# Head sums with a stationary selector in four column groups, and both directions' rates on two row halves

## The chip, the cores and the metric

The kernel runs on one core of a Trainium2 chip. It is one program for the whole inference step, launched once. The metric is the device time of one execution in microseconds (us): 2121.82 us is the median of three runs of the kernel before (2121.23 to 2124.61). The engines are called PE (TensorE, matrix multiplication), DVE (VectorE), ACT (ScalarE), POOL (GpSimd) and SP (SyncE, which here only starts transfers).

## The reference, cut to what matters

The program computes a two-layer trunk over 640 tokens (128 of context and 512 latent ones) of width 1024: layer 0 mixes tokens by attention and a state-space scan, layer 1 by RWKV-7 time mixing, and each is followed by a gated feed-forward block. The change lies in layer 1, in the part that makes the inputs of the recurrent scan. Cut to that:

```python
k  = einsum('btd,de->bte', xk, w_k)                    # xk, xw, xa, xr, xg, xv: six mixes of neighbouring tokens
kk = split_heads(k * k_k)                              # 16 heads of 64 channels
kk = kk * rsqrt(sum(kk * kk, axis=-1) + 1e-12)         # unit keys: one sum per token and head
a  = sigmoid(a0 + einsum(einsum(xa, a1), a2))          # rates, for both directions (j = 0, 1)
k_dir = split_heads(k * (1 + (a - 1) * k_a))           # a key per direction
r  = einsum('btd,de->bte', xr, w_r)
bonus = sum(r * k_dir * r_k, axis=(direction, -1)) * v # the other sum per token and head
```

The two sums over the 64 channels of a head are called head sums here: sums of squares (norms) and bonus sums. There are 16 heads, so a tile of 128 channels holds two.

## The kernel before, in words

Tokens lie along the free axis: an activation is eight tiles of 128 channels by 640 tokens, and a matmul moves at most 512 columns, so the 640 tokens go in two blocks of 320 (`BLK`). The program is written in a tile framework: the kernel text allocates tiles from pools of fixed depth, a scheduler decides the order of instructions on each engine (it is not the written order), and each engine runs its own list in order, with semaphores between them. An fp32 matmul is two instructions on PE, so counts in the trace are twice those of the code.

The stage around the change has five parts, one behind the other on PE:

- Keys (lines 1309 to 1337). For each of eight channel tiles `dense` (line 401) makes k in 48 matmuls of 320 columns: the inputs are split into a high and a low part in a shorter format, so three products for each of eight inputs and two blocks. ACT copies the result out of PSUM twice, as `ks` (line 1318) and, scaled, as `kk` (line 1319), and squares kk into `sq` (line 1320). The norms of the tile before (`norms`, line 1305) are five matmuls: the squares of 128 tokens are the stationary operand, 128x128, and a selector with two columns (`sel2`: head 0, head 1) is moved. So the sums land with tokens on partitions, as `rsqrt` on DVE needs them. Between these stand matmuls of line 1267, a low-rank projection for the rates and then for the decays.
- Decays (line 1410): ten matmuls of 512 columns for direction 0, each read by a sigmoid on ACT (line 1411) and sent to DRAM. The mixes for the next projection are made meanwhile (`mix`: ACT line 1241, DVE lines 1242 and 1246, and `split`: ACT line 435, POOL line 436).
- r and rates (lines 1421 to 1442). For each tile `dense` makes r; `rates` of the tile before spreads the reciprocal norm over the channels (line 1374, stationary `sw`), multiplies (DVE line 1375), makes a for direction 0 and then for direction 1 (line 1381: contraction over 64 rows, rows 0 to 63 of `a2` and `ha` for direction 0, 64 to 127 for direction 1), applies tanh (ACT line 1385), sends keys to DRAM and leaves r times k_dir in `ks` (DVE line 1396). `bonus` (line 1401) takes the tile before that one: five matmuls with `ks` stationary and two columns of `srk` moved, all sums in one PSUM tile that DVE copies to `bon` at the very end (line 1463).
- Gate (line 1456): 16 matmuls of 320 columns, each pair copied by ACT and sent to DRAM.
- V projection (line 1709) and the scan. `right.close()` (line 1464) ends the life of the stage's pools. The scan's tile `ta` takes over SBUF that `ks` had, so its first writes (the load of constants, memsets, the loads of decays and keys) wait until the last reader of `ks` is done. The matmuls of the V projection fill PE while the scan is prepared.

PSUM is eight banks here: one for head sums (`ps_n`), one for transposes (`pg`), two for low-rank sums and four for the rest. `tmp()` gives one of four SBUF buffers of 128x640; `sw` has one.

Of the kernel before, what the change touches and what calls it, by code (L numbers as in the profile page):

```python
# [9 lines left out]
F32 = mybir.dt.float32  # L10
# [8 lines left out]
NT = 640  # L19
# [6 lines left out]
BLK = ((0, 320), (320, 640))  # L26
# [62 lines left out]
def _build(ctx, tc, I, O):  # L89
# [1105 lines left out]
    if True:  # L1195
# [91 lines left out]
        V.tensor_scalar(kac, vcol('rwkv_k_a', 0, 8), -1.0, 2.0, op0=ALU.mult, op1=ALU.add)  # L1287
        srk = l1a.tile([128, 8, 2], F32, name="srk")
# [7 lines left out]
        pn = ps_n.tile([128, 512], F32, name="pn", tag="n")  # L1296
# [6 lines left out]
        def norms(sq, m):  # L1303
            for b in range(5):
                T.matmul(pn[:, b * 16 + m * 2:b * 16 + m * 2 + 2], sq[:, b * 128:(b + 1) * 128], sel2, start=True, stop=True)
# [5 lines left out]
        for m in range(8):  # L1311
# [9 lines left out]
            if sqs:  # L1321
                norms(*sqs.pop())
            sqs.append((sq, m))
# [12 lines left out]
        norms(*sqs.pop())  # L1336
# [5 lines left out]
        a0c = l1a.tile([16, 128], F32, name="a0c")  # L1342
        load(a0c, I['rwkv_a0'][0].rearrange("d (k p) -> (d k) p", p=128))
        a0h = l1a.tile([128, 16], F32, name="a0h")

        def unit_keys():
            rkk = tmp("rkk")[:, 0:80]
            rsqrt(sqp, rkk, pn[:, 0:80], 80, 1.0, 1e-12)
# [20 lines left out]
        def rates(m, kt):  # L1369
# [7 lines left out]
            kds = []  # L1377
            for d in range(2):
                pa = [pd.tile([128, 512], F32, name=f"pa{b}", tag="d") for b in range(2)]
                for b, (c0, c1) in enumerate(BLK):  # L1380
                    T.matmul(pa[b][:, 0:320], a2[64 * d:64 * d + 64, m * 128:(m + 1) * 128], ha[64 * d:64 * d + 64, c0:c1],
                             start=True, stop=True)
# [16 lines left out]
        def bonus(m):  # L1399
            for b in range(5):  # L1400
                T.matmul(pnb[:, b * 16 + m * 2:b * 16 + m * 2 + 2], ks[:, m, b * 128:(b + 1) * 128], srk[:, m, :], start=True, stop=True)
# [21 lines left out]
        for m in range(8):  # L1423
# [7 lines left out]
            if m == 0:  # L1431
                selh, rk2 = unit_keys()
                pnb = ps_n.tile([128, 512], F32, name="pn", tag="n")
                gate = lora1(lora_in('rwkv_g1', 1), 5)
            else:
                if done:
                    bonus(done.pop())
                done.append(rates(*kts.pop(0)))
            for _ in range(2):
                next(dec, None)  # L1440
# [20 lines left out]
        for m in done:  # L1461
            bonus(m)
# [488 lines left out]
```

## Time and profile before

| | |
|---|---|
| median of three runs | 2121.82 us |
| profiled execution: its time, its span | 2116.96 us, 2115.2 us |
| mean granted TensorE clock | 0.943 |
| PE busy | 1950.7 us, 92% of the span |
| PE weight loads busy (beside PE) | 1785.1 us, 84% |
| DVE, ACT, POOL busy | 1447.0, 940.2, 560.6 us (68%, 44%, 27%) |
| the changed stage | 957 to 1260 us from the span's start |

The profile is one execution. A merged row of the timeline gives its start, the sum of the busy time of the instructions in it, the engine, the line, the operation with output and inputs, shapes, and their count; in brackets, how long the engine was idle before and which work ended that. Ends of matmuls are modelled and overlap the next start, so the price of a group on PE is read from its start to the start of the next group. The rest of the program is not touched.

### The profile page before, as it was taken

The page shows a single profiled execution, that of the slowest core. Times are in us where ns is not written, and L with a number is a line of the kernel's source. Part 1 is how long each engine was busy: PE and PEld are TensorE (multiplying, and loading weights), DVE is VectorE, ACT ScalarE, POOL GpSimd, SP SyncE. Part 2 cuts the span into 40 slices and gives each one's busy share as a digit, 9 for nine tenths or more (in the row PEclk, how much of TensorE's full clock was granted, in tenths as well). Part 3 has the DMA queues.
Part 4 walks back from the last instruction along what each step waited for, and adds up shares of the span by engine and source line. Part 5 has one row for each costly group of instructions (what it writes and reads, how often), then busy time and mean ns, then how long its engine had stood idle before and what let it go on. Part 6 is the DMA issues. An engine that isn't in the chain of part 4 may idle for free. (4 is left out here: it accounts for less than half of the span.)

```text
span 2115.2 us, 42931 instructions
## 1 busy us (share of the span) xinstructions
PE 1950.7 (92%) x17701; PEld 1785.1 (84%) x17701; DVE 1447.0 (68%) x2589; ACT 940.2 (44%) x1734; POOL 560.6 (27%) x510
## 2 busy tenths in 40 slices
PE   6999988999999999989999897877789999999998
PEld 5888766989999999969677786867779899999998
DVE  4474666467666758587676839889956787666675
ACT  4333454253433525355555343544463535344351
POOL 2111331002424326031234123313321025243330
PEclk8999999999999999989997988878889899999999
DMA  9764000422433524342466634425344322323221
GB/s 295 220 201 115 7 1 21 149 90 81 130 120 90 162 67 121 108 122 65 148 206 224 202 105 134 123 78 152 100 141 123 120 81 80 100 66 95 61 90 50
DMA packets 256408, 245.72 MB, mean 116 GB/s; under 512 B 27850, under 2 KB 217299, under 8 KB 256085
## 3 DMA queue, kind: packets, MB, share of 16 engines
q1 hardware_dynamic: 233076, 208.87, 32.9%
q0 software_dynamic: 5856, 21.01, 3.0%
q10 hardware_dynamic: 17280, 13.11, 2.0%
q8 instruction: 139, 2.28, 0.5%
q14 instruction: 57, 0.46, 0.1%
HBM read 203.76 MB, written 39.19 MB: 115 GB/s over the span
## 5 line engine op out<-in xcount | busy, mean ns | idle before, releaser
L979 DVE TENSOR_TENSOR ol<-wr,oh 128x512 fp32r<-128x512 f32 x344 | 316.1, 935 | 101.0 <-ACT oh L978 93.6
L978 ACT CAST oh<-wr 128x512 fp32r<-128x512 f32 x344 | 211.3, 619 | 307.1 <-PE d L1130 174.7
L1130 PE MATMUL d<-hid,oh 128*128 128x320 f32 x1312 | 291.3, 310 | 3.6 <-ACT hid L1027 2.5
L1130 PEld LDWEIGHTS d<-hid,oh 128*128 128x128 f32 x1312 | 220.5, 188 | 5.2 <-ACT hid L1027 3.2
L1130 PE MATMUL d<-hid,ol 128*128 128x320 f32 x656 | 203.0, 309 | 0.0
L443 DVE SCALAR_TENSOR_TENSOR x<-d,mod,x 128x128 f32<-128x128 f32 (+2 forms) x204 | 77.2, 433 | 141.6 <-PE d L1130 116.1
L1000 POOL TENSOR_TENSOR g<-wr 128x512 f32<-128x512 f32 x36 | 48.4, 1344 | 460.0 <-DMA wr<-in_ffn_w_up_dram 280.8
L1130 PEld LDWEIGHTS d<-hid,ol 128*128 128x128 f32 x656 | 123.6, 188 | 0.0
L401 PE MATMUL d<-hh,wh 128*128 128x320 f32 (+1 forms) x464 | 118.7, 328 | 3.5 <-ACT hh L435 1.6
L401 PE MATMUL d<-hl,wh 128*128 128x320 f32 (+1 forms) x464 | 114.2, 317 | 3.8 <-POOL hl L436 3.2
L401 PE MATMUL d<-hh,wl 128*128 128x320 f32 (+1 forms) x464 | 112.9, 315 | 0.0
L388 DVE TENSOR_TENSOR wl<-wr,wh 128x1024 fp32r<-128x1024 f32 (+1 forms) x57 | 70.1, 1230 | 56.9 <-ACT wh L386 56.4
L386 ACT CAST wh<-wr 128x1024 fp32r<-128x1024 f32 (+1 forms) x57 | 58.8, 1035 | 105.1 <-PE d L401 65.7
L401 PEld LDWEIGHTS d<-hh,wh 128*128 128x128 f32 (+1 forms) x464 | 79.7, 190 | 17.2 <-ACT at L1385 4.1
L401 PEld LDWEIGHTS d<-hl,wh 128*128 128x128 f32 (+1 forms) x464 | 79.2, 189 | 8.5 <-POOL hl L436 5.9
L1027 ACT CAST hid<-e 128x320 fp32r<-128x320 f32 x88 | 40.5, 460 | 101.4 <-DVE e L1045 100.9
L401 PEld LDWEIGHTS d<-hh,wl 128*128 128x128 f32 (+1 forms) x464 | 79.2, 189 | 1.6 <-DVE wl L388 0.6
L1534 PE MATMUL pS<-ar,ta 64*128 64x128 f32 x640 | 56.4, 311 | 21.4 <-POOL uv L1602 10.2
L1003 POOL TENSOR_TENSOR wr<-wr 128x512 f32<-128x512 f32 x36 | 50.6, 1409 | 84.9 <-DVE ol L979 57.0
L1534 PEld LDWEIGHTS pS<-ar,ta 64*128 64x128 f32 x640 | 48.5, 213 | 28.6 <-POOL uv L1602 11.1
L1005 POOL TENSOR_TENSOR wr<-wr 128x512 f32<-128x512 f32 x36 | 53.3, 1492 | 66.4 <-DVE ol L979 66.4
L1562 DVE TENSOR_TENSOR xt__11664<-ta 128x31 f32<-128x31 f32 (+15 forms) x155 | 66.4, 429 | 4.4 <-ACT ta L1760 0.2
(630 smaller groups left out, 5997.5 us busy)
## 6 DMA issues: line engine op xcount, KB each, us to landing
wt<-in_mod_w_dram SPq DMA_DIRECT2D x80, 512.0 KB, 4.3
wr<-in_ffn_w_gate_dram SPq DMA_DIRECT2D x44, 512.0 KB, 4.4
wr<-in_ffn_w_up_dram SPq DMA_DIRECT2D x44, 512.0 KB, 5.2
wr<-in_ffn_w_down_dram SPq DMA_DIRECT2D x44, 512.0 KB, 4.2
ta<-kbd SPq DMA_DIRECT2D x10, 1024.0 KB, 6.2
ar<-rkd SPq DMA_DIRECT2D x20, 512.0 KB, 5.6
wr<-in_ab_w_in_dram SPq DMA_DIRECT2D x16, 512.0 KB, 7.1
wt<-in_mod_w_dram SPq DMA_DIRECT2D x6, 1024.0 KB, 8.9
```

The costliest lines, as they stand in the source:

```text
L386: S.copy(wh, wr)
L388: V.tensor_sub(wl, wr, wh.bitcast(F32))
L401: T.matmul(ps[b][0:cn, 0:320], w[:, k, 0:cn], a[:, t0:t1], start=(k == 0 and i == 0), stop=(k == w.shape[1] - 1 and i == 2))
L443: V.scalar_tensor_tensor(out=x[:, k, c0:c1], in0=ps[b][:, c0 - 320 * b:c1 - 320 * b], scalar=mod[:, layer, v, gcol + k:gcol + k + 1], in1= ...
L978: S.copy(hi, src)
L979: V.tensor_tensor(out=lo, in0=src, in1=hi.bitcast(F32), op=ALU.subtract)
L1000: E.tensor_tensor(out=g3, in0=a11, in1=a21, op=ALU.add)
L1003: E.tensor_tensor(out=a11, in0=a11, in1=a21, op=ALU.add)
L1005: E.tensor_tensor(out=a12, in0=a12, in1=a11, op=ALU.add)
L1130: T.matmul(bank[:, 0:c1 - c0], p, q, start=i == 0 and z == 0, stop=i == n - 1 and z == 2)
L1534: T.matmul(pS[i][:, m], bk[r, g4 * 4 + m, :], ar[r, g4 * 4 + m], start=True, stop=True)
L1562: V.tensor_tensor(out=tv, in0=nu[:, j + 1:32, j:j + 1].to_broadcast([128, n, j + 1]), in1=wu[:, j:j + 1, 0:j + 1].to_broadcast([128, n, j ...
```

## The change

Head sums are turned round. `head_sums` makes the sums of four channel tiles at a time. The stationary operand is a selector padded to 32 columns (`sel32`; for the bonus `sr`, four such selectors with r_k in them); the data are moved, 320 columns at a time; the four tiles go to four column groups of the array (`tile_position=(0, 32*i)`), that is to partitions 0, 32, 64 and 96 of one PSUM bank. The sums then lie with heads on partitions, so ACT copies the bank to SBUF (`hs`), five transposes bring tokens back onto partitions, and two DVE copies pick the two real rows of every 32 and write them straight to `bon`; `pn` is now a view of `bon` in SBUF. It runs four times: norms after key tiles 3 and 7, bonus after five rates and at the end. The four squares of a group are kept in all four `tmp` buffers until then. `rates` allocates the PSUM tiles of both directions first and issues block 0 of both directions, then block 1 of both. The load of `a0c` moves into `unit_keys` and into a `tmp` buffer.

```diff
@@ -1285,6 +1285,9 @@
 
         kac = l1a.tile([128, 8], F32, name="kac")
         V.tensor_scalar(kac, vcol('rwkv_k_a', 0, 8), -1.0, 2.0, op0=ALU.mult, op1=ALU.add)
+        sel32 = l1a.tile([128, 32], F32, name="sel32")
+        G.memset(sel32, 0.0)
+        V.tensor_copy(sel32[:, 0:2], sel2)
         srk = l1a.tile([128, 8, 2], F32, name="srk")
         V.tensor_tensor(out=srk, in0=sel2.unsqueeze(1).to_broadcast([128, 8, 2]),
                         in1=vcol('rwkv_r_k', 0, 8).unsqueeze(2).to_broadcast([128, 8, 2]), op=ALU.mult)
@@ -1293,16 +1296,28 @@
 
         ks = l1b.tile([128, KT, NT], F32, name="ks")
         kk = xp.tile([128, KT, NT], F32, name="kk", tag="x")
-        pn = ps_n.tile([128, 512], F32, name="pn", tag="n")
+        pn = bon.rearrange("p b h -> p (b h)")
         ha = sqp.tile([128, NT], F32, name="ha", tag="ha", bufs=1)
         hw = [sqp.tile([128, NT], F32, name=f"hw{d}", tag="hl", bufs=2) for d in range(2)]
         for d in range(2):
             G.memset(hw[d][64:128, :], 0.0)
             G.memset(hw[d][64:65, :], 1.0)
 
-        def norms(sq, m):
-            for b in range(5):
-                T.matmul(pn[:, b * 16 + m * 2:b * 16 + m * 2 + 2], sq[:, b * 128:(b + 1) * 128], sel2, start=True, stop=True)
+        def head_sums(q, rows, dst, sums):
+
+
+            hs = sqp.tile([128, NT], F32, name="hs", tag="kt") if dst is pn and sums[0] is sel32 else tmp("hs")
+            for c0, c1 in BLK:
+                pb = ps_n.tile([128, 512], F32, name="pn", tag="n")
+                for i, (a, w) in enumerate(zip(rows, sums)):
+                    T.matmul(pb[32 * i:32 * i + 32, 0:320], w, a[:, c0:c1], start=True, stop=True, tile_position=(0, 32 * i))
+                S.copy(hs[:, c0:c1], pb[:, 0:320])
+            for b0, b1 in ((0, 4), (4, 5)):
+                pt = pg.tile([128, 512], F32, name="pt", tag="g")
+                for b in range(b0, b1):
+                    T.transpose(pt[:, (b - b0) * 128:(b - b0 + 1) * 128], hs[:, b * 128:(b + 1) * 128], ident)
+                V.tensor_copy(dst.rearrange("p (b m i) -> p b m i", b=5, i=2)[:, b0:b1, 4 * q:4 * q + 4],
+                              pt[:, 0:(b1 - b0) * 128].rearrange("p (b m r) -> p b m r", m=4, r=32)[:, :, :, 0:2])
 
         low = None
         nxt = mix(0, (hq, hp))
@@ -1318,9 +1333,10 @@
                 S.copy(ks[:, m, c0:c1], ps[b][:, 0:320])
                 S.activation(kk[:, m, c0:c1], ps[b][:, 0:320], AF.Copy, scale=vcol('rwkv_k_k', m))
             S.activation(sq, kk[:, m, :], AF.Square)
-            if sqs:
-                norms(*sqs.pop())
-            sqs.append((sq, m))
+            if len(sqs) == 4:
+                head_sums(0, sqs, pn, [sel32] * 4)
+                sqs = []
+            sqs.append(sq)
             for _ in range(2):
                 lps = next(low)
             if m == 3:
@@ -1333,19 +1349,19 @@
             if 1 <= m < 5:
                 take(nxt, (nhis, nlos), 1)
         take(nxt, (nhis, nlos), 4)
-        norms(*sqs.pop())
+        head_sums(1, sqs, pn, [sel32] * 4)
         his, los = nhis, nlos
 
 
 
         a2 = lora2(((0, 128, I['rwkv_a2'][0].rearrange("d r c -> (d r) c")),))
-        a0c = l1a.tile([16, 128], F32, name="a0c")
-        load(a0c, I['rwkv_a0'][0].rearrange("d (k p) -> (d k) p", p=128))
         a0h = l1a.tile([128, 16], F32, name="a0h")
 
         def unit_keys():
+            a0c = tmp("a0c")[0:16, 0:128]
+            load(a0c, I['rwkv_a0'][0].rearrange("d (k p) -> (d k) p", p=128))
             rkk = tmp("rkk")[:, 0:80]
-            rsqrt(sqp, rkk, pn[:, 0:80], 80, 1.0, 1e-12)
+            rsqrt(sqp, rkk, pn, 80, 1.0, 1e-12)
             pt = [pg.tile([128, 512], F32, name="pt", tag="g") for _ in range(1)]
             rkt = tmp("rkt")[0:16]
             for b in range(4):
@@ -1375,11 +1391,14 @@
                 V.tensor_tensor(out=kk[:, m, c0:c1], in0=pb[:, 0:320], in1=kk[:, m, c0:c1], op=ALU.mult)
             nc.gpsimd.dma_start(out=rkd[:, m, :, 0, :], in_=kk[:, m, :].rearrange("p (c t) -> p c t", c=10))
             kds = []
+
+            pas = [[pd.tile([128, 512], F32, name=f"pa{b}", tag="d") for b in range(2)] for d in range(2)]
+            for b, (c0, c1) in enumerate(BLK):
+                for d in range(2):
+                    T.matmul(pas[d][b][:, 0:320], a2[64 * d:64 * d + 64, m * 128:(m + 1) * 128], ha[64 * d:64 * d + 64, c0:c1],
+                             start=True, stop=True)
             for d in range(2):
-                pa = [pd.tile([128, 512], F32, name=f"pa{b}", tag="d") for b in range(2)]
-                for b, (c0, c1) in enumerate(BLK):
-                    T.matmul(pa[b][:, 0:320], a2[64 * d:64 * d + 64, m * 128:(m + 1) * 128], ha[64 * d:64 * d + 64, c0:c1],
-                             start=True, stop=True)
+                pa = pas[d]
                 at = tmp("at")
                 for b, (c0, c1) in enumerate(BLK):
                     S.activation(at[:, c0:c1], pa[b][:, 0:320], AF.Tanh, bias=a0h[:, d * 8 + m:d * 8 + m + 1], scale=0.5)
@@ -1396,9 +1415,12 @@
             V.tensor_tensor(out=ks[:, m, :], in0=kt, in1=ks[:, m, :], op=ALU.mult)
             return m
 
-        def bonus(m):
-            for b in range(5):
-                T.matmul(pnb[:, b * 16 + m * 2:b * 16 + m * 2 + 2], ks[:, m, b * 128:(b + 1) * 128], srk[:, m, :], start=True, stop=True)
+        def bonus(q):
+            ms = range(4 * q, 4 * q + 4)
+            sr = sqp.tile([128, 4, 32], F32, name="sr", tag="sw", bufs=1)
+            G.memset(sr, 0.0)
+            G.tensor_copy(sr[:, :, 0:2], srk[:, 4 * q:4 * q + 4])
+            head_sums(q, [ks[:, m] for m in ms], pn, [sr[:, i] for i in range(4)])
 
         def decays():
             for d in range(2):
@@ -1430,12 +1452,11 @@
             kts.append((m, kt))
             if m == 0:
                 selh, rk2 = unit_keys()
-                pnb = ps_n.tile([128, 512], F32, name="pn", tag="n")
                 gate = lora1(lora_in('rwkv_g1', 1), 5)
             else:
-                if done:
-                    bonus(done.pop())
                 done.append(rates(*kts.pop(0)))
+                if len(done) == 5:
+                    bonus(0)
             for _ in range(2):
                 next(dec, None)
             lps = next(gate)
@@ -1458,9 +1479,7 @@
             for b, (c0, c1) in enumerate(BLK):
                 S.copy(kt[:, c0:c1], pa[b][:, 0:320])
             nc.scalar.dma_start(out=gd[m], in_=kt)
-        for m in done:
-            bonus(m)
-        V.tensor_copy(bon.rearrange("p b h -> p (b h)"), pnb[:, 0:80])
+        bonus(1)
         right.close()
```

The scheduler's order changes with it. On PE, near the middle of the key projection (fifth channel tile), before, with `d` the key sums, `pn` the norms and `l` the low-rank sums:

```order
L401 MATMUL d_10161<-hh,wl 128x320
L401 MATMUL d_10162<-hh,wl 128x320
L1305 MATMUL pn<-ca,sq 128x2 x5
L1267 MATMUL l_10127<-u,wr 128x320
L1267 MATMUL l_10128<-u,wr 128x320
L1267 MATMUL l_10127<-u,wr 128x320
L1267 MATMUL l_10128<-u,wr 128x320
```

Such a piece follows each key tile. On PE at the same place of the changed kernel (`sel_9692` is `sel32`, `pt` the transposed sums):

```order
L401 MATMUL d_10054<-hh,wl 128x320
L1313 MATMUL pn<-sq,sel_9692 32x320 x4
L1267 MATMUL l_10131<-u,wr 128x320
L1267 MATMUL l_10132<-u,wr 128x320
L1267 MATMUL l_10131<-u,wr 128x320
L1267 MATMUL l_10132<-u,wr 128x320
L1313 MATMUL pn<-sq,sel_9692 32x320 x4
L1318 MATMUL pt<-ca,hs 128x128 x2
L401 MATMUL d_10165<-hh,wh 128x320
```

The five matmuls of a tile are gone here; four tiles' sums stand in two groups of four with the low-rank matmuls between, and the transposes follow among the next tile's `d` (two at once, two and one further on). At key tiles 1 to 3 nothing stands in their place.

On PE, between two tiles of r, before (`pa` are the rates, `pb` the spread norms, `pw` the decays of direction 1):

```order
L1401 MATMUL pn<-srk,ks 128x2 x5
L1374 MATMUL pb<-rk_10599,sw 128x320 x2
L1267 MATMUL l_10624<-u,wr 128x320
L1381 MATMUL pa_10823<-ha,wr 128x320
L1381 MATMUL pa_10824<-ha,wr 128x320
L1381 MATMUL pa_10836<-ha,wr 128x320
L1381 MATMUL pa_10837<-ha,wr 128x320
L1267 MATMUL l_10625<-u,wr 128x320
```

Rates of direction 0 (`pa_10823`, `pa_10824`) stand ahead of those of direction 1. On PE at the same place of the changed kernel, where `pa_10823` and `pa_10824` are direction 0 and `pa_10825` and `pa_10826` direction 1:

```order
L401 MATMUL d_10761<-hh,wl 128x320
L1390 MATMUL pb<-rk_10605,sw 128x320 x2
L1267 MATMUL l_10630<-u,wr 128x320
L1398 MATMUL pa_10823<-ha,wr 128x320
L1398 MATMUL pa_10825<-ha,wr 128x320
L1398 MATMUL pa_10824<-ha,wr 128x320
L1398 MATMUL pa_10826<-ha,wr 128x320
L1432 MATMUL pw<-wr,hw_9702 128x512
```

The bonus sums are gone from here, and the second and third rate have changed places.

On PE, at the end of the gate (line 1456 before, 1477 after), before (`pz` is the V projection, line 1709 before, 1728 after):

```order
L1456 MATMUL pa_11617<-gt__11479,wr 128x320
L1401 MATMUL pn<-srk,ks 128x2 x5
L1456 MATMUL pa_11618<-gt__11479,wr 128x320
L1709 MATMUL pz<-wh,hh 128x256
L1709 MATMUL pz<-wh,hl 128x256
```

The last tile's bonus sums stand one gate matmul ahead of the V projection. And changed, where the gate ends:

```order
L1477 MATMUL pa_11617<-gt__11479,wr 128x320
L1313 MATMUL pn<-ks,sr 32x320
L1477 MATMUL pa_11618<-gt__11479,wr 128x320
L1728 MATMUL pz<-wh,hh 128x256
L1728 MATMUL pz<-wh,hl 128x256
```

Only the last of the four tiles' first blocks is left at this place; the other three stand further up among the gate's matmuls. On PE, 26 rows of `pz` further on in the changed kernel:

```order
L1728 MATMUL pz<-wh,hh 128x256
L1728 MATMUL pz<-wh,hl 128x256
L1313 MATMUL pn<-ks,sr 32x320 x4
L1318 MATMUL pt<-ca,hs 128x128 x2
L1728 MATMUL pz<-wl,hh 128x256
```

The last readers of `ks` are now the four matmuls of that second block, behind 26 matmuls of the V projection; before, they stood ahead of its first one. From the scan on, the order of every engine is as before.

## Rows read from the trace of the kernel before

**Rows 1.** Busy time by stretch: busy PE, PEld, DVE, ACT, POOL; clock, DMA share, GB/s.

```profile
957.30:1012.30 55.00, 55.00 (x350) 50.88 (x348) 38.01 (x50) 32.54 (x56) 5.69 (x4) 1.00 0.18 54
1012.30:1028.50 16.20, 11.79 (x32) 4.96 (x31) 9.74 (x12) 11.91 (x20) 6.14 (x4) 0.89 0.46 152
1028.50:1131.10 102.60, 99.76 (x554) 82.15 (x552) 70.64 (x105) 57.09 (x95) 33.44 (x36) 0.95 0.65 200
1131.10:1158.40 27.30, 25.65 (x82) 15.86 (x82) 20.50 (x22) 16.78 (x33) 12.30 (x12) 0.69 0.67 228
1158.40:1192.30 33.90, 28.06 (x275) 25.32 (x274) 23.52 (x27) 10.52 (x20) 8.61 (x12) 1.00 0.82 253
1228.70:1260.40 31.70, 30.39 (x425) 29.86 (x426) 2.45 (x2) 16.28 (x22) 3.95 (x6) 0.84 0.14 39
```

**Rows 2.** Timeline of PE at the end of a key tile.

```profile
957.36 1.17 PE L1305 MATMUL pn<-ca,sq 128*128 128x2 f32 x10
958.39 2.40 PE L1267 MATMUL l<-u,wr 128*128 128x320 f32 x8
960.39 0.69 PE L401 MATMUL d<-hh,wh 128*128 128x320 f32 x2
```

**Rows 3.** Line 1305 alone: durations in ns, first and last start in us.

```profile
L1305 PE MATMUL pn<-ca,sq x80: 166/251/251, 947.1 to 1014.2; 128*128 128x2 f32 x80
```

**Rows 4.** Timeline of PE, another stage: four column groups of 32 (line 235).

```profile
70.70 1.50 PE L235 MATMUL pa<-wt,sT 128*32 128x256 f32 x24
72.14 0.41 PE L401 MATMUL d<-hh,wh 128*128 128x320 f32 x1
```

**Rows 5.** Timeline of ACT behind the key tile of rows 2.

```profile
957.26 1.05 ACT L386 CAST wh<-wr 128x1024 fp32r<-128x1024 f32 x1 [1.00 <-PE d L401]
959.26 0.55 ACT L1319 ACTIVATE kk<-d,vec 128x320 f32<-128x320 f32 x1
```

**Rows 6.** Timeline of PE: four transposes (line 1352) and what follows.

```profile
1037.66 0.60 PE L1352 MATMUL pt<-ca,rkk 128*16 128x128 f32 x4
1038.10 0.70 PE L1267 MATMUL l<-u,wr 128*128 128x320 f32 x2
```

**Rows 7.** Timeline of PE in the decays of direction 0.

```profile
1022.59 6.47 PE L1410 MATMUL pw<-wr,hw 128*128 128x512 f32 x10 [4.18 <-ACT th L1411]
```

**Rows 8.** Timeline of ACT in the decays of direction 0.

```profile
1015.34 1.28 ACT L1411 ACT_TABLE_LOAD   x1
1020.50 0.83 ACT L1241 ACTIVATE mx<-hx,cm 128x642 f32<-128x642 f32 x1 [1.64 <-POOL hl L436]
```

**Rows 9.** Timeline of PE between r tiles: a rate, a bonus sum, a bonus sum that waits.

```profile
1048.54 1.35 PE L1381 MATMUL pa<-ha,wr 64*128 64x320 f32 x8
1049.83 0.81 PE L1267 MATMUL l<-u,wr 128*128 128x320 f32 x2
...
1059.77 1.17 PE L1401 MATMUL pn<-srk,ks 128*128 128x2 f32 x10
1060.88 0.56 PE L1374 MATMUL pb<-rk,sw 64*128 64x320 f32 x2
...
1104.60 1.77 PE L1401 MATMUL pn<-srk,ks 128*128 128x2 f32 x10 [0.97 <-DVE ks L1396]
```

**Rows 10.** Timeline of ACT between r tiles.

```profile
1062.94 1.06 ACT L1385 ACTIVATE at<-pa,a0h 128x320 f32<-128x320 f32 x2 [1.56 <-PE pa L1381]
```

**Rows 11.** Timeline of PE from the stage's end into the V projection.

```profile
1157.04 1.17 PE L1401 MATMUL pn<-srk,ks 128*128 128x2 f32 x10
1158.07 0.79 PE L1456 MATMUL pa<-gt__11479,wr 128*128 128x320 f32 x2
...
1158.81 0.28 PE L1709 MATMUL pz<-wh,hl 128*128 128x256 f32 x1
1158.93 0.28 PE L1709 MATMUL pz<-wl,hh 128*128 128x256 f32 x1
```

**Rows 12.** Timeline of SP's queue at the start of the scan.

```profile
1158.89 0.35 SPq L103 DMA_DIRECT2D ta<-in_cst_c_dram  x1
```

## What the change was predicted to do

> **What bounds the kernel now.** I read the page's first part and then its slices: PE is busy for 92% of the span, so an instruction taken off PE counts where PE is what the others wait for, and nowhere else. Next I cut the changed stage into stretches by what PE does [rows 1]. In the key projection (957.3 to 1012.3) PE is busy in all 55.00 us: it is the bound. In the decays of direction 0 (to 1028.5) it is busy for 11.79 of 16.20 us and waits for ACT, 4.18 us within one group of ten [rows 7]. In r and rates (to 1131.1) it is busy for 99.76 of 102.60 us, but at a granted clock of 0.95, and some of that busy time is ends that stretch over waits. In rest and gate (to 1158.4) the clock is 0.69 and the PE, DVE and ACT chains are mixed. Behind that the scan is prepared: PE is idle for 5.84 us of the first 33.90, and at the end (1228.7 to 1260.4) PE is the bound again, 30.39 of 31.70 us with DVE at 2.45. Then I read the timeline of PE at the places where a sum stands.
>
> **Prices.** A tile's norms are ten instructions from 957.36 to 958.39, 1.03 us [rows 2], and there are 80 instructions for eight tiles, the last ones at 1014.2 [rows 3]: seven tiles lie in the key projection, one in the decays. A bonus sum takes 1.11 us (1059.77 to 1060.88) where it doesn't wait [rows 9]. The new blocks don't occur before; the nearest thing is line 235 of the other stage, also four column groups with 32 stationary columns and 128 rows: 24 instructions from 70.70 to 72.14, 1.44 us, with the change of shape at both ends in it [rows 4]. That is 0.06 us per instruction of 256 columns; eight instructions of 320 columns come to 8 x 0.06 x 320/256 = 0.60 us per block. From the other side: a matmul instruction of 128 rows and 320 columns alone takes (960.39 - 958.39) / 8 = 0.25 us [rows 2], so eight one after the other would be 2.00 us. I take 0.60, since line 235 is the same form. A transpose takes (1038.10 - 1037.66) / 4 = 0.11 us [rows 6], five 0.55 us.
>
> The Trainium skill (TensorEngine Tiling (Array Packing), Tiling Modes, Key Properties) says that tiles operate independently, but also that changing the tiling mode drains the array. No row here shows a drain by itself; the 1.44 us hold two such changes.
>
> **Key projection.** Seven norms go: -7 x 1.03 = -7.21 us. One call of head sums comes: two blocks 1.20, transposes 0.55. One wait is new, since all sums share one PSUM bank: the second block needs the first block's copy on ACT. PE reaches it 0.60 + 2.00 = 2.60 us after the key tile's end. ACT has the key tile's evictions first, the last of which ends at 959.26 + 0.55 = 959.81, 2.45 us behind 957.36 [rows 5], and then the copy, at most 0.53 us (half of the 1.06 us of two tanh of the same shape [rows 10]): ready at about 2.9 to 3.0, so PE waits for 0.3 to 0.4. Queued behind it on PE are two transposes and the next key tile. The transposes wait for the second copy, then for the single bank `pt`; dense matmuls stand between them, so I add 0.2. Sum: 1.20 + 0.55 + 0.4 + 0.2 = 2.35, net -4.9 us. Bounds: -5.5 (no waits) and -2.1 (blocks at 2.00 us).
>
> **Decays of direction 0.** The eighth norm goes and the second call comes, while PE waits for ACT. ACT gets two more copies, about 0.9 us together, ahead of its sigmoids; the DVE copies and the rsqrt stand among the mixes. ACT had a gap of 1.64 us there [rows 8] in which the copies may hide, and PE's -1.03 + 1.75 lies inside its wait of 4.18. I take +0.9. Bounds: 0 (hidden in the gap) and +3 (the mix chain gives way to both copies and a table load of 1.28 us [rows 8] is repeated).
>
> **r and rates.** Five bonus sums of this stretch go: -5 x 1.11 = -5.55, and a wait of 0.97 for DVE ahead of one [rows 9]. One call comes: 1.20 + 0.55 + 0.6 for its waits, since its first block is split 1 + 3 by a low-rank matmul, +2.35. That makes -3.2 without the wait, -4.2 with it. Not all of it is PE's to give: behind the sum stand the spread norms, the rates and their tanh, and the PSUM banks of the next tile come free only with those. ACT waits for PE there (1.56 us [rows 10]), which speaks for a gain; DVE's multiply (line 1375) and the chain of tanh, scaling and `ks` don't get shorter. I take -2.3, two thirds; bounds 0 and -4.2.
>
> The new order of the rates is worth nothing by the trace: eight instructions of 64 rows take 1049.83 - 1048.54 = 1.29 us [rows 9], 0.16 each, where instructions one after the other take 0.25. So the two directions already run beside each other although direction 0 is written first. The floor of four pairs at 0.25 is 1.00; bounds 0 and -8 x 0.29 = -2.3, and I take 0, because what follows is the tanh of direction 0, whose second block now comes a place later.
>
> The Trainium skill (TensorE: Matmul & The Clock Gate, Part 3) says the opposite of why that should be so: matmuls stay strictly in program order, only weight loads are pulled ahead. By that the old order would let just one pair of four meet, which is the rival on the rates below; the 1.29 us don't agree with it.
>
> **Rest and gate.** Three bonus sums (at the least 1.03 each, 1158.07 - 1157.04 [rows 11]) go, and the first block of the last call comes in three pieces between gate matmuls (2 + 1 + 1), of which each costs up to 0.5: -3.1 + 1.5. The stretch goes by its chains, with a clock of 0.69, so I count 0; bounds -1.5 and +2.
>
> **Start of the scan.** The load of the scan's constants went out at 1158.89 [rows 12], as soon as the last bonus sum was done with `ks`. Now its last reader stands behind 26 matmuls of V at 1158.93 - 1158.81 = 0.12 us [rows 11], 3.1 us, plus the block's 0.60: the preparation begins about 3.7 us later, less the 1.0 that the last bonus sum took before V. Queued behind that are the memsets on POOL, the loads of decays and keys on SP, and with them DVE. Against it, PE has done more of V by then (26 matmuls and what fills the longer wait), so that the last stretch, which PE bounds, is shorter by as much. I take 0; bounds -1 and +3.5 (V's advance is worth nothing).
>
> **Sum.** -4.9 + 0.9 - 2.3 + 0 + 0 + 0 = -6.3, taken as -6 us. Against the profiled execution (2116.96 us, of which 2115.2 is its span and 1.8 lies around it) that is 2111. The profiled execution is 4.9 us below the median of the three runs, which I take as a difference between executions: 2121.8 - 6 = 2116 us for the median.
>
> **Rivals.**
> All PE work counts: every removed instruction comes off the end. Keys -4.9, eighth norm -1.0 + 1.75, r -4.2, rates -2.3, gate -1.5, block and transposes in V +1.15: -11, 2111 us. For it: PE at 55.00 of 55.00 us in the keys and 99.76 of 102.60 in r. Against: the 4.18 us wait in the decays and the clock of 0.69 in the gate show stretches that PE doesn't set.
> The rates halve: if PE kept to the written order, direction 0's two blocks would follow each other in the same rows, and only its second would run beside direction 1's first: three turns of 2 x 0.25 = 0.50 us, 1.50, against two turns now, 1.00. That is 8 x 0.5 = -4 more, -10, 2112 us. Against: 1.29 us is less than three turns [rows 9].
> The gain is given back at ACT and at the scan's start: decays +2, r and rates -1, scan +2, with keys -4.9: -2, 2120 us. For it: one bank for all sums, ACT in the middle of every call, and `ks` held by 3.7 us longer. Against: ACT waits for PE in r, and the last stretch is PE's.
> The Trainium skill (TensorEngine Tiling (Array Packing), PSUM Bottleneck) warns of just that: tiling speeds up the matmuls, not the copies out of PSUM. The 0.4 us wait worked out above is how it would show.
> Slower: the four column groups don't run beside each other when each has its own moving data and its own stationary tile. The place is each of the eight blocks, the price 2.00 instead of 0.60, 8 x 1.4 = +11: with the rest, -6 + 11 = +5, 2127 us. It decides once a block takes over 0.60 + 6/8 = 1.35 us. Against: in line 235 each group has its own moving data, too, though the same stationary columns [rows 4].
> Slower at the scan: it begins 3.7 us later, nothing of V's advance is regained, and the decays cost +3 with r at 0: -4.9 + 3 + 3.5 = +1.6, 2123 us. Against: the idle 5.84 us of PE and the PE-bound end in [rows 1].
>
> **Chances.** Forecast 0.44, all of PE's work 0.10, rates 0.04, given back 0.27, column groups in turn 0.06, scan 0.09. A difference under 0.2%, 4.2 us, can't be told from none. The forecast's own range is -9 to -3 us, some four fifths of it over 4.2: 0.36 faster and 0.08 same. With the first two rivals (0.14) and a little of the third (0.03) faster is 0.53; same is 0.08 + 0.24 + 0.04 of the scan's case = 0.36; slower is 0.06 + 0.05 = 0.11. The range reaches from the first rival with 1.5 us for the spread of medians, 2109.5, to 2122.5, where the scan's case begins.
>
> **What would show it.** Key projection: from the first to the last dense matmul about 4.9 us shorter, each block of eight instructions at about 0.6, a wait of some 0.4 for ACT ahead of one block. Decays: as long or 0.9 longer. r and rates: the first tiles 0.9 shorter each, the tile with the new call longer. Rates: eight instructions still in about 1.3 us. Scan: its constants' load 3 to 4 us later relative to V's first matmul, and a shorter last stretch. It is wrong if blocks take 2 us, if rates fall to 1.0 or below with the tile's time, or if the stretch from 1158 to 1260 grows by more than 1 us.

## The result, and the profile after

The changed kernel takes 2106.1 us (median of four runs, 2097.93 to 2108.86), the kernel before 2122.9 us beside it: 16.8 us less. The ratio of the executions taken beside each other is 0.9912, 95% interval 0.9889 to 0.9934, that is 18.7 us less (14 to 23.6). The forecast was 2116.0 us, range 2109.5 to 2122.5: the sign was right, the size was not, and the time lies below the range. A second, independent timing of the same kernel gave 2103.36 us and 0.9912 (0.9891 to 0.9932).

Its profiled execution has a span of 2107.0 us, against 2115.2 before. The first view is the busy time by stretch, cut at the same work in both kernels: keys and decays; r tiles 1 to 5; r tiles 6 to 8; gate; V projection up to the scan's first transposes; scan preparation; end of V up to the scan's first state matmul. Columns as in [rows 1]. Before:

```profile
942.46:1028.49 86.03, 81.62 (x469) 69.40 (x469) 61.78 (x79) 55.30 (x93) 13.41 (x9) 0.98 0.24 75
1028.49:1095.10 66.61, 65.18 (x367) 52.28 (x365) 47.58 (x75) 38.19 (x64) 19.20 (x21) 1.00 0.65 193
1095.10:1135.39 40.29, 38.36 (x207) 32.27 (x207) 26.90 (x36) 22.19 (x37) 16.87 (x18) 0.87 0.60 195
1135.39:1158.45 23.06, 21.93 (x66) 13.49 (x66) 16.71 (x19) 13.50 (x28) 9.67 (x10) 0.63 0.75 262
1158.45:1164.03 5.58, 4.71 (x39) 4.46 (x37) 0.04 (x1) 0.43 (x1) 1.24 (x4) 1.00 0.76 268
1164.03:1228.70 64.67, 55.09 (x485) 52.05 (x485) 56.84 (x96) 20.73 (x35) 7.37 (x8) 0.97 0.62 187
1228.70:1260.37 31.67, 30.36 (x425) 29.83 (x425) 2.45 (x2) 16.28 (x22) 3.92 (x6) 0.84 0.14 39
```

And after:

```profile
946.71:1030.19 83.48, 78.92 (x432) 62.00 (x431) 61.17 (x83) 56.01 (x96) 13.75 (x9) 0.98 0.25 76
1030.19:1094.91 64.72, 62.35 (x337) 48.31 (x335) 48.91 (x74) 38.47 (x64) 19.31 (x21) 1.00 0.66 196
1094.91:1129.59 34.68, 32.65 (x197) 26.42 (x197) 26.21 (x39) 22.16 (x38) 16.99 (x20) 1.00 0.70 229
1129.59:1149.44 19.85, 16.78 (x53) 8.50 (x53) 12.89 (x17) 14.13 (x29) 10.66 (x12) 0.91 0.84 278
1149.44:1158.46 9.02, 8.61 (x72) 7.68 (x71) 0.36 (x2) 1.92 (x5) 1.22 (x4) 1.00 0.78 266
1158.46:1224.26 65.80, 56.59 (x495) 53.97 (x496) 57.08 (x97) 21.17 (x35) 6.28 (x8) 0.95 0.60 183
1224.26:1252.25 27.99, 26.14 (x393) 25.62 (x393) 2.19 (x2) 14.97 (x21) 4.07 (x6) 0.82 0.12 37
```

The differences are -2.55, -1.89, -5.61, -3.21 and, over the last three together, +0.89: -12.37 us in the stage. The reader should look at the third and fourth row of each: there the granted clock was 0.87 and 0.63 before and is 1.00 and 0.91 after. Seven tenths of the stage's gain (8.82 us) lie in these two rows, for which the forecast had a part of its -2.3 at most. The work ahead of the stage, which the change doesn't touch, took 4.25 us longer in the execution after (the first rows begin at 942.46 and 946.71); that is why the spans differ by 8.2 only.

The call of head sums in the key projection, timeline of PE and, in the last row, of ACT, answers to [rows 2]:

```profile
980.03 0.75 PE L1313 MATMUL pn<-sq,sel 128*32 128x320 f32 x8
980.71 1.35 PE L1267 MATMUL l<-u,wr 128*128 128x320 f32 x4
982.75 1.34 PE L1267 MATMUL l<-u,wr 128*128 128x320 f32 x4 [0.70 <-DVE u L1246]
984.02 0.74 PE L1313 MATMUL pn<-sq,sel 128*32 128x320 f32 x8
984.70 0.44 PE L1318 MATMUL pt<-ca,hs 128*128 128x128 f32 x2
984.90 0.54 PE L401 MATMUL d<-hh,wh 128*128 128x320 f32 x2
...
983.03 0.44 ACT L1314 COPY hs<-pn 128x320 f32<-128x320 f32 x1
```

A block takes 980.71 - 980.03 = 0.68 us; 0.60 was forecast from [rows 4], and 2.00 would have been the price in turn. A transpose takes 0.10. The wait is not for ACT's copy but for the mixes on DVE: with the norms gone PE comes to the low-rank matmul before its input is there. The copy was done at 983.47, 0.55 us ahead of the second block; without the wait of 0.70 PE would have come to that block 0.15 us ahead of it.

The rates, to be compared with [rows 9]:

```profile
1050.03 1.35 PE L1398 MATMUL pa<-ha,wr 64*128 64x320 f32 x8
1051.45 1.13 PE L1432 MATMUL pw<-wr,hw 128*128 128x512 f32 x2
```

Eight instructions go by with the same 1.35 us of busy time as before; in rates_only below they take 1.28 us up to the next group, and 1.29 before. The start of the scan, SP's queue, answers to [rows 12]:

```profile
1153.68 0.35 SPq L103 DMA_DIRECT2D ta<-in_cst_c_dram  x1
```

It goes out 4.24 us behind V's first matmul, and 0.44 us behind it before: 3.8 later.

### The profile page after: what moved, and what is told of

The parts are those of the page before. It is cut to its first block, busy times and chain, and to the rows that moved or that the text cites. A ratio compares the mean times of both kernels' runs of the same rounds, so it can differ in the third digit from the quotient of the medians.

```text
span 2107.0 us, 42812 instructions
## 1 busy us (share of the span) xinstructions
PE 1940.9 (92%) x17625; PEld 1767.9 (84%) x17625; DVE 1433.5 (68%) x2597; ACT 941.8 (45%) x1742; POOL 563.4 (27%) x515
## 5 line engine op out<-in xcount | busy, mean ns | idle before, releaser
L979 DVE TENSOR_TENSOR ol<-wr,oh 128x512 fp32r<-128x512 f32 x344 | 304.7, 902 | 103.9 <-ACT oh L978 96.0
L1553 PEld LDWEIGHTS pS<-ar,ta 64*128 64x128 f32 x640 | 51.2, 227 | 28.4 <-POOL ar L1540 12.4
## 6 DMA issues: line engine op xcount, KB each, us to landing
wt<-in_mod_w_dram SPq DMA_DIRECT2D x6, 1024.0 KB, 10.5
```

What stands on the lines that cost most here:

```text
L979: V.tensor_tensor(out=lo, in0=src, in1=hi.bitcast(F32), op=ALU.subtract)
L1553: T.matmul(pS[i][:, m], bk[r, g4 * 4 + m, :], ar[r, g4 * 4 + m], start=True, stop=True)
```

## Experiments

Three theories were on the table. Queue: the bonus sums cost what they take on PE and what waits behind them. Clock: the sums in their old form go with a low granted clock from the sixth r tile on, and the rest of the stage pays for it. Rates: the new order lets the two directions run side by side. Ratios are against the kernel before on the same chip.

**One part at a time.**

```diff
 rates_only: the kernel before with
-            for d in range(2):
-                pa = [pd.tile(...) for b in range(2)]
+            pas = [[pd.tile(...) for b in range(2)] for d in range(2)]
+            for b, (c0, c1) in enumerate(BLK):
+                for d in range(2):
+                    T.matmul(pas[d][b][:, 0:320], ...)
 norms_only: head_sums(0 and 1, sqs, ...) new, bonus(m) and rates as before
 bonus_only: bonus(0), bonus(1) through head_sums, norms(sq, m) and rates as before
 rates_undone: the changed kernel with the rates as before
```

rates_only: 

> Only the order of the rates is changed (block 0 of both directions, then block 1). Theory PE queue (the bonus sums stood in PE's queue ahead of other work, and taking them out is the gain): -1 to +1 us, eight instructions of the rates still in about 1.3 us. Theory rates (the written order kept the halves apart): -4 us, the eight instructions in about 1.0 us. Theory clock (the gain is the granted clock between the fourth r tile and the gate, which was 0.63 to 0.91 before and 1.00 or 0.91 after, and goes with less work on PE): 0 us, the clock there as low as before.

norms_only: 

> Only the norms go through the new head sums; bonus sums and rates as before. All theories: the key projection 2 to 3 us shorter by the profile after (one call costs some 3.3 us of the 1.1 us per tile that are saved), the decays about as long. PE queue: -2 to -4 us. Clock: the same, if the clock stays low from the fourth r tile on; some 5 us more if it is 1.00 there.

bonus_only: 

> Only the bonus sums go through the new head sums; norms and rates as before. PE queue: -8 to -10 us, wherever the clock stands. Clock: -8 to -10 us if the clock is 1.00 from the fourth r tile to the gate, -3 to -4 us if it is as low as before. Theory rates: -4 to -6 us.

rates_undone: 

> The changed kernel with the rates in the order of before: both kinds of head sums new. PE queue and clock: as the changed kernel, -12 to -17 us against before. Theory rates: 4 us above that, -8 to -13 us.

| | median us | ratio | interval |
|---|---|---|---|
| rates_only | 2122.1 | 1.0008 | 0.9998 to 1.0019 |
| norms_only | 2115.52 | 0.9981 | 0.9965 to 0.9996 |
| bonus_only | 2107.74 | 0.9942 | 0.9928 to 0.9956 |
| rates_undone | 2101.22 | 0.9911 | 0.9896 to 0.9926 |

The rates are worth nothing: alone they change nothing that can be measured, and taking them back loses nothing. That theory falls. The norms are worth 4.0 us (0.8 to 7.4), the bonus sums 12.3 us (9.3 to 15.3), and both parts together come to about the whole. So the miss is in the bonus sums. In bonus_only the stretches of r tiles 1 to 5, 6 to 8 and gate are:

```profile
1030.09:1094.50 64.41, 62.27 (x336) 48.64 (x335) 49.56 (x74) 37.81 (x63) 18.71 (x21) 1.00 0.64 189
1094.50:1129.95 35.45, 33.44 (x198) 26.56 (x198) 26.18 (x39) 22.06 (x38) 17.17 (x20) 1.00 0.68 224
1129.95:1149.62 19.67, 15.40 (x52) 7.45 (x53) 12.72 (x17) 14.04 (x29) 10.49 (x12) 1.00 0.84 280
```

The clock is 1.00 throughout. In rates_only, whose bonus sums are the old ones, it is 0.85, 0.90 and 0.87 in r tiles 6 to 8 and 0.63 in the gate, as before.

**The sums taken away, put back, and put back in another form.**

```diff
 no_bonus: the kernel before; in bonus(m) five matmuls for m == 7 only, each with all 16 columns of srk
 bonus_late: the kernel before
-                if done:
-                    bonus(done.pop())
+                if len(done) > 1:
+                    bonus(done.pop(0))
 thin: the changed kernel, ahead of rates(...) in five places
+                    pq = ps_n.tile([128, 512], F32, name="pq", tag="n")
+                    for b in range(5):
+                        T.matmul(pq[:, 2 * b:2 * b + 2], ks[:, done[-1], b * 128:(b + 1) * 128], srk[:, done[-1], :], ...)
 wide: the same places
+                    for c0, c1 in BLK:
+                        T.matmul(pq[:, 0:320], ident, ks[:, done[-1], c0:c1], ...)
```

no_bonus: 

> The kernel before with the bonus sums left out but for one group of five matmuls at the end (the bonus term isn't computed). Theory queue (only the PE time of the sums and the wait behind them count): at most 7 x 1.11 + 0.97, -5 to -9 us, the granted clock between the fourth r tile and the gate 0.63 to 0.91 as before. Theory clock (the sums in their old form bring the clock down there): clock 1.00 in all these stretches and -12 to -16 us.

bonus_late: 

> The kernel before with each bonus sum one r tile later, so that ks has long been written; the same instructions. Theory wait (the sums held PE's queue up until DVE had written ks): -2 to -8 us. Theory clock: 0 to -1 us, the clock as low as before. Theory queue: 0 to -1 us.

thin: 

> The changed kernel with five useless groups added between the r tiles, each five matmuls in the old form of the bonus sums (a tile of ks stationary, two columns moved, 1.1 us), written to PSUM and not read. Theory queue: 5 x 1.1 = +3 to +6 us against the changed kernel, -11 to -15 against before, clock 1.00. Theory clock: the clock falls again from the fourth r tile to the gate (0.6 to 0.9), and the time is -3 to -7 us against before, 10 to 13 above the changed kernel.

wide: 

> The same as the run with the useless groups of two columns, but each group is two matmuls of 320 columns with the identity stationary: about the same time on PE (4 x 0.25 = 1.0 us), other form. Theory queue: the same +3 to +6 us against the changed kernel. Theory clock: the clock stays at 1.00 between the fourth r tile and the gate, and the time is +0 to +5 us against the changed kernel, clearly below the run with two columns.

| | median us | ratio | interval |
|---|---|---|---|
| no_bonus | 2112.59 | 0.9958 | 0.9943 to 0.9973 |
| bonus_late | 2121.46 | 1.0001 | 0.9987 to 1.0015 |
| thin | 2111.33 | 0.9954 | 0.9940 to 0.9968 |
| wide | 2118.53 | 0.9982 | 0.9968 to 0.9996 |

Leaving the old sums out altogether gains 8.9 us, not the 12 to 16 of the clock theory, although the clock is 1.00 in all r tiles. Giving each sum a tile's time more changes nothing: it took the wait of 0.97 us for DVE [rows 9] down to 0.61, and the clock fell all the same (0.88, 0.88 and 0.85 in r tiles 6 to 8). The five groups of thin cost some 9 us by the ratios against the changed kernel with the clock at 1.00 in all r tiles (it fell behind the last of them, 0.9 us into the gate), and the wide ones cost more than the thin ones, the reverse of the forecast; in wide the scheduler put the groups elsewhere, PE waited 1.45 us for DVE once, and the clock was 0.91 in that r tile. Neither theory comes out of these four as written: the adding of work moves other work.

**The form alone, at the old places.**

```diff
 before_wide: the kernel before, in bonus(m) (wide_r: for m < 6 only; wide_gate: for m >= 6 only)
-            for b in range(5):
-                T.matmul(pnb[:, b * 16 + m * 2:b * 16 + m * 2 + 2], ks[:, m, b * 128:(b + 1) * 128], srk[:, m, :], ...)
+            for c0, c1 in BLK:
+                T.matmul(pnb[:, 0:320], ident, ks[:, m, c0:c1], start=True, stop=True)
 thin8: the changed kernel with useless groups as in thin at eight places, two of them in the gate
```

before_wide: 

> The kernel before with each bonus sum replaced, at its place, by two matmuls of 320 columns with the identity stationary (about 1.0 us on PE instead of 1.1; the bonus term isn't computed). Theory form (it is the two-column form that brings the granted clock down after the fourth r tile): clock 1.00 there, -5 to -8 us. Theory timing (the clock falls by what the whole stretch leaves PE to do, whatever the form): the clock at 0.6 to 0.9 as before, -1 to +1 us.

thin8: 

> The changed kernel with eight useless groups in the old form (five matmuls, two columns) at about all the places where the bonus sums stood, the gate among them. Theory form: the clock falls after the fourth r tile as in the kernel before, and nearly all of the gain goes: -6 to -2 us against before. Theory PE time: the clock stays, 8 x 1.1 us of which some two thirds show, +4 to +8 against the changed kernel, -8 to -13 against before.

wide_r: 

> The kernel before with the six bonus sums that stand between r tiles and at their end (tiles 0 to 5) replaced by two matmuls of 320 columns; the two in the gate (tiles 6 and 7) stay in the old form (the bonus term isn't computed). If the two-column groups bring the clock down by their number in a stretch, it is 1.00 in r and near that in the gate, which has only two: -8 to -11 us. If the gate's clock falls for its own waits, it is 0.6 to 0.85 there all the same, -5 to -8 us.

wide_gate: 

> The other half: the six sums between r tiles in the old form, the two in the gate replaced by matmuls of 320 columns (the bonus term isn't computed). If the old form counts where it stands, r is as before (0.84, 0.91, 0.87 from the sixth tile on) and the gate's clock above 0.63: -1 to -4 us. If the gate matters more, -5 to -8 us.

| | median us | ratio | interval |
|---|---|---|---|
| before_wide | 2111.58 | 0.9948 | 0.9932 to 0.9964 |
| thin8 | 2118.74 | 0.9975 | 0.9962 to 0.9988 |
| wide_r | 2112.48 | 0.9957 | 0.9941 to 0.9973 |
| wide_gate | 2114.33 | 0.9977 | 0.9960 to 0.9993 |

A wide group takes 1.16 us on PE, a thin one 1.11. Still the kernel before gets 11 us faster when its eight groups are wide. The same three stretches (r tiles 1 to 5, 6 to 8, gate) of before_wide:

```profile
1033.26:1099.15 65.89, 65.89 (x343) 51.27 (x341) 43.35 (x68) 35.43 (x59) 17.69 (x20) 1.00 0.63 195
1099.15:1136.27 37.12, 37.12 (x198) 29.39 (x196) 30.01 (x41) 23.22 (x39) 17.56 (x19) 1.00 0.66 211
1136.27:1157.09 20.82, 17.50 (x51) 10.08 (x51) 16.09 (x19) 14.79 (x31) 11.31 (x10) 0.84 0.69 245
```

And of thin8, which has the changed kernel's sums and eight thin groups besides:

```profile
1031.36:1099.88 68.52, 66.95 (x367) 52.58 (x365) 49.31 (x75) 38.45 (x64) 18.76 (x21) 0.98 0.63 189
1099.88:1141.18 41.30, 37.33 (x230) 30.19 (x230) 30.50 (x43) 22.45 (x38) 17.61 (x20) 0.92 0.61 197
1141.18:1165.03 23.85, 22.46 (x72) 13.98 (x70) 11.45 (x13) 14.25 (x29) 10.02 (x11) 0.71 0.70 251
```

Both ways the clock goes with the form: 1.00 in r where the groups are wide, 0.98, 0.92 and 0.71 where thin ones are put back, and with them some 13 us of the gain go by the ratios (0.9975 for 0.9912), in which the 8 x 1.11 = 8.9 us that the groups take on PE are a part. wide_r has 1.00 in r and 0.84 in the gate and gives 9.1 us (5.7 to 12.5); wide_gate has 0.91 in r tiles 6 to 8 and 0.76 in the gate and gives 4.9 us (1.5 to 8.5), of which its gate shows 1.4 (21.63 us). So the groups between r tiles seem to matter more, for the gate behind them too (20.83 us in wide_r), but the two intervals overlap.

Two reservations stay. The 11 us of before_wide are not the clock's alone: in its profile the three stretches are 6.1 us shorter than before, but the V projection and the scan preparation take 4.1 back, the whole stage is only 0.2 to 1.4 us shorter than in the two profiles of the kernel before, and the scan took 378.56 us for 384.88 and 385.66. And the scheduler moved a few instructions with the form, so that PE has no waits in r in the wide kernels (65.89 of 65.89 us busy): form and waits changed together.

The kept traces tell the two apart. Here are a wait of PE, the start of the old sum behind it and what follows; an old sum without a wait, and what follows; both in the kernel before:

```profile
1103.60:1104.60 1.00, 0.03 (x2) 0.00 (x1) 1.00 (x3) 0.00 (x0) 0.26 (x1) 1.00 0.00 0
1104.60:1105.20 0.60, 0.60 (x6) 0.60 (x6) 0.60 (x2) 0.28 (x1) 0.00 (x0) 1.00 0.00 0
1105.22:1112.03 6.81, 6.81 (x23) 4.71 (x24) 3.23 (x6) 3.24 (x8) 1.00 (x1) 0.50 0.74 176
...
1059.77:1060.88 1.11, 1.11 (x13) 1.09 (x11) 0.00 (x0) 1.11 (x2) 0.00 (x0) 1.00 0.00 0
1060.88:1067.70 6.82, 6.82 (x30) 4.48 (x30) 5.33 (x9) 5.21 (x11) 1.81 (x3) 1.00 0.74 172
```

And a longer wait with no sum behind it, and what follows, in no_bonus:

```profile
1103.10:1104.40 1.30, 0.05 (x1) 0.05 (x1) 1.30 (x4) 0.13 (x1) 0.00 (x0) 1.00 0.00 0
1104.40:1111.30 6.90, 6.90 (x41) 5.87 (x42) 6.76 (x11) 5.43 (x11) 1.75 (x3) 1.00 0.79 199
```

In r of all eight profiles with thin groups there (before, before_again, rates_only, norms_only, bonus_late, wide_gate, thin, thin8), 24 of the 46 groups have a wait of PE of 0.44 us or more that ended at most 2.2 us ahead of them: behind 20 of these the clock fell, 0.6 to 2.7 us after the group's start. Behind the 22 others it never fell. Waits of up to 1.31 us without a thin group left it at 1.00 in r; the exceptions are wide, with its wait of 1.45, and rates_undone, where it fell 0.26 us ahead of the gate. So neither the old form alone nor a wait of that length alone brought the clock down in r; the two close together did, 20 times of 24.

**Repeats, and one attempt to go further.**

```diff
 gate_split: the changed kernel, gate loop
-                S.copy(kt[:, c0:c1], pa[b][:, 0:320])
+                (S.copy if b == 0 else V.tensor_copy)(kt[:, c0:c1], pa[b][:, 0:320])
```

after_again: 

> The changed kernel once more, for its spread: -15 to -20 us against before; the stretch from the first low-rank matmul to the scan's first state matmul 305 to 307 us against 317 to 318, the clock from the fourth r tile to the gate 1.00. If that repeats, the time that the stage doesn't explain (some 4 to 5 us) should be found outside it.

gate_split: 

> The changed kernel with the second copy of each gate tile on DVE instead of ACT. Theory DVE chain (the gate ends when DVE has written the last ks, and DVE is held up by POOL): 0 to +2 us against the changed kernel. Theory ACT (the gate's copies on ACT are its bound): -2 to -3 us against the changed kernel.

before_again: 

> The kernel before once more, for a second profile: the same stretches within 0.3 us up to the scan, the clock 0.84, 0.91, 0.87 and 0.63 in the same places; the scan (the first state matmul to the end of the mixing's output) 385 to 389 us if the remaining 4 us of the gain lie there as a rule, 382 to 384 if they are chance.

after_third: 

> The changed kernel a third time: the stage as in its two other profiles (305 to 306.5 us); the scan 382 to 384 us if the remaining 4 us are a rule, else anything from 382 to 389.

gate_split took 2103.04 us (0.9915, 0.9891 to 0.9939), the changed kernel beside it 2103.36: no gain is seen from taking half of the gate's copies off ACT, though by the intervals 2 or 3 us can't be excluded, and no version here clearly beats the changed kernel. The stage of the changed kernel was 306.04 and 306.22 us in the two further profiles (305.54 in the first), that of the kernel before 316.74 (317.91). before_again (one execution) is the cleanest measure of what the clock costs at one place, because it is the same program. Timeline of PE ahead of the seventh r tile there:

```profile
1107.28 1.28 PE L1401 MATMUL pn<-srk,ks 128*128 128x2 f32 x10 [0.99 <-DVE ks L1396]
1108.41 0.79 PE L1267 MATMUL l<-u,wr 128*128 128x320 f32 x2
1109.13 1.35 PE L1381 MATMUL pa<-ha,wr 64*128 64x320 f32 x8
```

The same place in the first profile of the kernel before, whose first row is the last of [rows 9]:

```profile
1106.23 1.42 PE L1267 MATMUL l<-u,wr 128*128 128x320 f32 x2
1107.57 2.51 PE L1381 MATMUL pa<-ha,wr 64*128 64x320 f32 x8
```

The same instructions behind the same wait take 1.13, 0.72 and 1.35 us in one execution and 1.63, 1.34 and 2.51 (busy) in the other: one is at the level of 2.4 GHz, the other, from 0.6 us into the sums on, at 1.2. The whole gap to the next r tile is 5.50 us at a clock of 1.00 and 7.62 at 0.68. In before_again the clock fell a tile later instead (0.90 and 0.84 in the last two), so that r tiles 6 to 8 took 39.09 us and not 40.29. It falls in both, and not at the same place.

## Why the prediction was right and wrong

**Right: the new blocks and the transposes.** 0.68 us for 0.60, 0.10 for 0.11. The rival that the column groups run in turn is out.

**Right: the rates.** 0 was forecast; rates_only measured +0.08% (-0.02 to +0.19). The rival in which the rates halve falls with it: the old order takes 1.29 us and the new one 1.28. The Trainium skill (TensorE: Matmul & The Clock Gate, Part 3) has matmuls in strict program order; by that the old order would have taken three turns, an estimate of 1.5 us, and the 1.29 us don't agree with it.

**Right: the scan's start.** Its first load is 3.8 us later against V's first matmul (3.7 forecast), and the last stretch is 3.68 us shorter (27.99 for 31.67), as V had come further: +0.89 in all for 0.

**Half wrong: the key projection.** Its end, before and after:

```profile
1012.35 1.10 PE L1410 MATMUL pw<-wr,hw 128*128 128x512 f32 x2
...
1013.07 0.74 PE L1313 MATMUL pn<-sq,sel 128*32 128x320 f32 x6
```

From 942.46 and 946.71 that is 69.89 us before and 66.36 after, -3.53 for "-4.9 us". The rest of the first view's row, the decays, measures 16.14 and 17.12, +0.98 for "+0.9" (the 4.18 us of [rows 7] are a wait ahead of the ten matmuls, not within them). The term that was wrong is the wait. Where the norms went, PE waited twice for the mixes on DVE, 0.70 and 0.69 us (one of them in the rows of the result): before, PE had no such wait in the key projection. The forecast looked for the new wait at ACT's copy, where there was none, and had 0.4 for it. Both together are -2.55; four other profiles of kernels with the new norms (norms_only, rates_undone, after_again, after_third) have -2.67, -2.37, -1.64 and -1.55 against the same 86.03. The timed norms_only, 4.0 (0.8 to 7.4), can't tell these from the forecast's -4.0, so that its agreement with it is luck.

**Wrong: "r and rates" at -2.3 and "rest and gate" at 0.** They measure -1.89 - 5.61 = -7.50 and -3.21 (cut where the gate begins, 4.29 us behind the forecast's cut). The sums' own part was sized well: r tiles 1 to 5 hold three old sums of 1.11 us and gave 1.89 us, where two thirds were forecast. What failed is the step that took the granted clock of [rows 1] (0.95 in r and rates, 0.69 in rest and gate) as a property of the place. I read the clock as an argument against a gain there ("the clock of 0.69 in the gate show stretches that PE doesn't set"), when it was something that the sums brought with them where PE had just waited. What full clock would have given in r tiles 6 to 8 is an estimate, put together from the two profiles of the kernel before: 12.79 + 11.57 + 11.53 = 35.9 us instead of 40.29 and 39.09 (tile 6 of before_again; tile 7 with the dense part of 7.40 from before_again; tile 8, whose dense part ran at full clock in neither, with tile 6's 7.30; their gaps of 4.17 and 4.23 from the first profile). So against the first profile 4.4 us of the 5.61 are clock, against the second 3.2 of 4.41, and 1.2 are the sums less the call. In the gate the split isn't as clean: it is 19.9 us in all three profiles of the changed kernel at 0.91, 0.83 and 0.83, 20.8 in before_wide and wide_r at 0.84, and 23.1 and 23.4 before at 0.63 and 0.71; it goes with what r leaves behind as well as with its own sums, and how much of its 3.21 us is clock isn't shown.

**What stays open.** The stage gives 10.5 to 12.4 us in the profiles, the timing 16.8 and 19.5. A part of that is which executions were profiled: they took 2116.96 and 2120.51 us before, 2108.86, 2100.5 and 2108.93 after, 12.6 apart in the mean. Of these the stage makes 11.4. Some 2 us lie behind the mixing: from its end to the last feed-forward matmul it is 460.7 and 461.6 us before and 459.05, 459.06 and 459.18 after, in work that the change doesn't touch. The scan in between is 384.88 and 385.66 us before and 386.47, 381.98 and 384.59 after, so no rule there. The 4 to 7 us between 12.6 and the timings weren't located. Nor is it settled why 4 of the 24 thin groups behind a wait left the clock up; three of the four are at the same place, ahead of the seventh r tile, where in other executions it fell.

## What to carry to other kernels

A low granted clock in a stretch is a cost like any other, and an edit can remove it: ask which instructions stand in the stretch where it falls, and price the whole stretch at both levels before costing the edit. When PE work is removed from a stretch in which PE is busy throughout, look one step up for the next input that is late (here the mixes on DVE, not the new copy on ACT). And a suspicion about a form is best tested by the form alone at the old place, since added or removed instructions make a scheduler move others; even then, look whether the waits moved with it.

## What was not expected of the hardware

The clock fell in r in all seven profiles of kernels with six to eight thin groups in r and gate (first in the fourth, sixth or seventh r tile; down to 0.63 in the gate), among long dense matmuls with PE busy for 38.36 of 40.29 us; in ten others, with no thin group between r tiles or with the five of thin, it was 1.00 in all r tiles (once 0.99). The exception is wide, where it fell to 0.91 and 0.97 behind a wait of 1.45 us. In the key projection the same thin form, seven times in 55 us in which PE never waited, left the clock at 1.00 [rows 1]; between r tiles it fell behind 20 of the 24 thin groups that had a wait of PE of 0.44 us or more just ahead of them, and behind none of the 22 others. Two executions of one program lost it at places one r tile apart, at a difference of 1.2 us.
